# Moving a norm gain from the own inputs into the streamed weights, loading every input cast, and starting seven tiles together in PSUM

## The chip, the cores and the metric

One Trainium2 chip; the program runs on all 8 cores, four on each of two dies. Time is device time of the slowest core, in microseconds (us). Engines are named as in the profile: PE (TensorE; PEld its weight loads), DVE (VectorE), ACT (ScalarE), POOL (GpSimd), SP (SyncE, which only issues DMA here).

In a *slow* run one die has a visibly lower granted clock and the time is longer: in the first comparison, for one, die 1 at 0.887 to 0.896 and die 0 at 0.985 to 0.987, against all cores at 0.985 to 0.988.

## The reference, cut to what matters

```python
xn   = rmsnorm(x, g_in)                          # (x / rms(x)) * g_in
proj = einsum('bsd,de->bse', xn, w_in)           # 4096 -> 11840 columns
gB, gC, h, z_conv, c_q, c_kv, k_rope, z_attn = split(proj)
# gated short convolution from gB, gC, h, z_conv; latent attention from c_q, c_kv, k_rope, z_attn
out  = rmsnorm(x + concat(y_conv, y_attn) @ w_out, g_final)
```

Batch 2, sequence 4096, width 4096, fp32 in and out. Each core owns 1024 frames of one batch element. It needs `c_kv` and `k_rope` (512+64 columns, weights `WC`) for all 4096 frames of its batch element, as keys: 32 *tiles* of 128 frames, of which 8 are its *own*. All the other columns of `proj` it needs for its own frames alone: 88 *streamed weight tiles* of 4096x128. The row scale 1/rms(x) is applied after the matmuls. The gain `g_in` runs along the contracted dimension, so it can be multiplied into either x or the weights.

## The kernel before: the parts that matter

The kernel lists its instructions for each engine in program order, and in the traces each engine takes its own list in that order: in the changed kernel, on core 2, DVE stood 5.3 us for a table, up to 122.1 us, while an addition behind it in its list, whose input ACT had written by 110.5 us, started at 122.9 us. A helper derives the waits from what is read and written. One of its rules: an engine that reads a PSUM bank also waits for earlier reads of that bank by other engines.

```python
for k in rc:                                   # cells read; PSUM cells are whole banks
    ...
    if k[0] == "ps":
        for e2, r in c.r.items():              # other engines that have read this bank
            if e2 != eng:
                need(r)
```

First stage: every tile gives latent and rope columns and its sum of squares. `WC` is key weight times `g_in`. Other tiles (`a != 0`) are cast to bf16 by the DMA itself (`load("pool", ...)`). Own tiles come as fp32 through three small stages, because they are needed twice: cast, for the keys, and multiplied by `g_in`, as `XG`, for the streamed weights.

```python
def prep(T, c):                                # quarter c of tile T
    a, m = TILES[T]
    xt = xb[T % 4][:, 8 * c:8 * c + 8, :]
    src = xt
    if a == 0:                                 # own tile
        s = xst[nst[0] % 3]                    # three fp32 stages
        load("sp", s, x_tile[T, quarter c])
        tt(XG[own columns], s, g_in, ALU.mult) # DVE
        src = s
        act(xt, src, AF.Copy)                  # ACT: fp32 -> bf16
    act(q, src, AF.Square)                     # ACT
    tt(q[:, 0:512], q[:, 0:512], q[:, 512:1024], ALU.add)     # DVE: sums of squares,
    tt(o[:, :], q[:, 0:256], q[:, 256:512], ALU.add)          # reduced further by PE

def pe_main(T, kc):
    A, B = banks_of(T)                         # a pair of PSUM banks
    mm(psum[:, A, 0:256], x_, WC[:, kc, 0:256], kc == 0, kc == 31)
    mm(psum[:, B, 0:320], x_, WC[:, kc, 256:576], kc == 0, kc == 31)
```

Four other tiles run together while `WC` arrives. Then own and other tiles alternate (eight pairs), and other tiles close the stage. `post(T)` normalizes, `pe_trans(T)` transposes into the key buffers.

Second stage: streamed weights, cast on load into three buffers.

```python
def wload(i):
    for c in range(2):
        load("pool", WS[i % 3][half c], w_in_d[i, half c])
# 64 tiles of the convolution group, then 8 of c_q, then 16 of z_attn; the c_q part:
for m in range(8):
    for hf in range(2):
        for kc in range(32):
            mm(o, w[:, kc, :], XG[:, kc, c0:c0 + 512], kc == 0, kc == 31)
            if kc == 15 and pend:
                pend.pop(0)()                  # PE: ones x squares of the previous half
        ts(CQG[...], o, g_q, ALU.mult)         # DVE reads the bank
        act(s2, o, AF.Square)                  # ACT reads the same bank, after DVE
        pend.append(lambda: mm(bank(6 + hf), ones16, s2, ...))
    wload(64 + m + 3)
```

Attention and the output projection follow. The change doesn't touch them.

The softmax here doesn't subtract the row's maximum and nothing guards it: scores larger than these inputs give would overflow.

Of the kernel before, what the change touches and what calls it, by code (L numbers as in the profile page):

```python
# [15 lines left out]
D = 4096  # L16
# [68 lines left out]
class Prog:  # L85
# [15 lines left out]
    def add(self, eng, fn, reads=(), writes=(), dma=False):  # L101
# [23 lines left out]
        for k in wc:  # L125
            c = self.cells.get(k)
            if c is None:
                c = self.cells[k] = Cell()
            w = c.w
            if w is not None and (dma or w.dma_sem is not None or w.eng != eng or eng != "pe"):  # L130
                need(w)
            for e2, r in c.r.items():
                if dma or e2 != eng or eng == "pool":
                    need(r)
            for r in c.dr:
                need(r)
# [109 lines left out]
KB = 1024  # L246
# [15 lines left out]
def tile_order():  # L262

    own = [(0, t) for t in range(8)]
    oth = [(a, m) for a in (1, 2, 3) for m in range(8)]
    seq = oth[:4]
    rest = oth[4:]
    for t in range(8):
        seq += [own[t], rest[t]]
    return seq + rest[8:]  # L270
# [5 lines left out]
def build_program():  # L276
# [7 lines left out]
    x_tile = din("x_tile", [32, 128, 4096])  # L284
# [21 lines left out]
    with stack:  # L306
# [62 lines left out]
        def small(name, shape, dt=F32):  # L369
# [12 lines left out]
        stat = [small("stat%d" % i, [8]) for i in range(4)]  # L382
        fst = [small("fst%d" % i, [12]) for i in range(8)]
# [16 lines left out]
              enumerate((Z_R + 8 * KB, Z_R + 16 * KB, Z_Q + 36 * KB, Z_RB + 4352))]  # L400
        xst = [sb("xst%d" % i, o, [8, 128], F32) for i, o in enumerate((Z_R, Z_R + 4 * KB, Z_G + 28 * KB))]
        wst = [sb("wst%d" % i, Z_C + i * 4608, [2, 576], F32, Z_K2) for i in range(7)]
        sq = [sb("sq%d" % i, Z_T + i * 2 * KB, [1024], BF16) for i in range(2)]
        sa2 = [sb("sa2_%d" % i, Z_T + 4 * KB + i * 512, [256], BF16, Z_CONST) for i in range(6)]
        zc = [Z_RB + 4352 + 8 * KB]

        def ptmp(name, shape, dt=F32):
            n = int(np.prod(shape)) * (2 if dt == BF16 else 4)
            t = sb(name, zc[0], shape, dt, Z_T)
            zc[0] = (zc[0] + n + 63) // 64 * 64  # L410
            return t

        ckn = [ptmp("ckn%d" % i, [512], BF16) for i in range(2)]
        junk = ptmp("junk", [512], BF16)
        kr = [ptmp("kr%d" % i, [2, 64], BF16) for i in range(2)]
        ckn += [sb("ckn%d" % (2 + i), Z_K2 + 5 * KB + i * KB, [512], BF16) for i in range(2)]
        kr += [sb("kr%d" % (2 + i), Z_K2 + 7 * KB + i * 256, [2, 64], BF16) for i in range(2)]
        t1 = ptmp("t1", [64])
        t2 = ptmp("t2", [64])
        cst = [ptmp("cst%d" % i, [128]) for i in range(3)]  # L420
        gkv = ptmp("gkv", [512])

        def load_other(T, parts=2):
            n = 32 // parts
            for c in range(parts):
                load("pool", xb[T % 4][:, c * n:(c + 1) * n, :],
                     x_tile[T, :, c * n * 128:(c + 1) * n * 128].rearrange("p (k t) -> p k t", k=n))

        def load_cs(T):
            load("sp", cst[T % 3][:, :], cs_key[T])  # L430

        nsa = [0]
        nst = [0]
        saof = {}

        def prep(T, c):

            a, m = TILES[T]
            xt = xb[T % 4][:, 8 * c:8 * c + 8, :]
            src = xt  # L440
            if a == 0:
                s = xst[nst[0] % 3]
                nst[0] += 1
                load("sp", s[:, :, :], x_tile[T, :, c * 1024:(c + 1) * 1024].rearrange("p (k t) -> p k t", k=8))
                tt(XG[:, 8 * c:8 * c + 8, m * 128:(m + 1) * 128], s[:, :, :],
                   g_in[:, 8 * c:8 * c + 8].unsqueeze(2).to_broadcast([128, 8, 128]), ALU.mult)
                src = s[:, :, :]
                act(xt, src, AF.Copy)  # L448
            q = sq[nsa[0] % 2]
            o = sa2[nsa[0] % 6]  # L450
            saof[(T, c)] = o
            nsa[0] += 1
            act(q[:, :].rearrange("p (k t) -> p k t", k=8), src, AF.Square)
            tt(q[:, 0:512], q[:, 0:512], q[:, 512:1024], ALU.add)
            tt(o[:, :], q[:, 0:256], q[:, 256:512], ALU.add)

        def banks_of(T):
            return (2 * T, 2 * T + 1) if T < 4 else (2 * ((T - 4) % 3), 2 * ((T - 4) % 3) + 1)

        def pe_main(T, kc):  # L460
            A, B = banks_of(T)
            x_ = xb[T % 4][:, kc, :]
            mm(psum[:, A, 0:256], x_, WC[:, kc, 0:256], kc == 0, kc == 31)  # L463
            mm(psum[:, B, 0:320], x_, WC[:, kc, 256:576], kc == 0, kc == 31)  # L464

        def pe_ssq(T, c):
            B = banks_of(T)[1]
            s = saof[(T, c)]
            for j in range(2):
                mm(psum[:, B, 320:321], s[:, j * 128:(j + 1) * 128], ones16[:, 0:1], False, True)  # L470
            if TILES[T][0] == 0:
                for j in range(2):
                    mm(psum[:, B, 384:512], ones16[:, :], s[:, j * 128:(j + 1) * 128], False, True)

        def post(T):
            a, m = TILES[T]
            A, B = banks_of(T)
            st = stat[T % 4]
            cs = cst[T % 3]
            sx = psum[:, B, 320:321]  # L480
            lat = psum[:, A:A + 2, 0:256]
            act(junk[:, :].rearrange("p (b c) -> p b c", b=2), lat, AF.Square, accum=st[:, 0:1])
            act(st[:, 2:3], sx, AF.Sqrt, scale=1.0 / D, bias=EPSA)
            if a == 0:
                act(RB[:, m * 128:(m + 1) * 128], psum[:, B, 384:512], AF.Sqrt, scale=1.0 / D, bias=EPSA)
            ts(st[:, 1:2], sx, EPS / D, ALU.mult, EPS * EPS, ALU.add)
            recip(st[:, 4:5], st[:, 2:3])
            act(st[:, 3:4], st[:, 0:1], AF.Sqrt, scale=1.0 / 512, bias=st[:, 1:2])
            stt(t1[:, :], psum[:, B, 256:320], st[:, 4:5], cs[:, 0:64], ALU.mult, ALU.mult)
            stt(t2[:, :], psum[:, B, 256:320], st[:, 4:5], cs[:, 64:128], ALU.mult, ALU.mult)  # L490
            recip(st[:, 5:6], st[:, 3:4])
            stt(ckn[T if T < 4 else T % 2][:, :].rearrange("p (b c) -> p b c", b=2), lat, st[:, 5:6],  # L492
                gkv[:, :].rearrange("p (b c) -> p b c", b=2), ALU.mult, ALU.mult)
            k_ = kr[T if T < 4 else T % 2]
# [4 lines left out]
            if a == 0:  # L499
                recip(RB[:, m * 128:(m + 1) * 128], RB[:, m * 128:(m + 1) * 128])  # L500
            if T + 3 < 32:
                load_cs(T + 3)

        def pe_trans(T):
            a, m = TILES[T]
            b_ = 6 + T % 2
            pt = psum[:, b_, :].bitcast(BF16)
            for j in range(4):
                tr(pt[:, j * 128:(j + 1) * 128], ckn[T if T < 4 else T % 2][:, j * 128:(j + 1) * 128], id16[:, :])
            tr(pt[:, 512:640], kr[T if T < 4 else T % 2][:, :, :].rearrange("p a b -> p (a b)"), id16[:, :])  # L510
# [8 lines left out]
        for c in range(8):  # L519
            for T in range(4):  # L520
                load("pool", xb[T][:, 4 * c:4 * c + 4, :],
                     x_tile[T, :, c * 512:(c + 1) * 512].rearrange("p (k t) -> p k t", k=4))
        for i in range(16):
            w = wst[i % 7]
            load("sp", w[:, :, :], w_ckv_d[i].rearrange("p (k c) -> p k c", k=2))
            for j in range(2):
                ts(WC[:, 2 * i + j, :], w[:, j, :], g_in[:, 2 * i + j:2 * i + j + 1], ALU.mult)
            if i == 1:
                idst = sb("idst", Z_K2, [128])
                gmst = sb("gmst", Z_K2 + 512, [2, 64])  # L530
                load("sp", idst[:, :], ident_d)
                load("sp", gmst[:, :, :], gmask_d.rearrange("p (a b) -> p a b", a=2))
                load("sp", g_q[:, :], g_q_d)
                load("sp", convw[:, :], convw_d)
                load("sp", gkv[:, :], g_kv_d)
                ms(ones16[:, :], 1.0)
                ms(eps_t[:, :], EPS)
        cp(id16[:, :], idst[:, :])
        cp(gmask[:, :, :], gmst[:, :, :])
        for T in range(3):  # L540
            load_cs(T)


        for c in range(4):
            for kc in range(8 * c, 8 * c + 3):
                for T in range(4):
                    pe_main(T, kc)
            if c:
                for T in range(4):
                    pe_ssq(T, c - 1)  # L550
            for T in range(4):
                prep(T, c)
            for kc in range(8 * c + 3, 8 * c + 8):
                for T in range(4):
                    pe_main(T, kc)
        for T in range(4):
            pe_ssq(T, 3)

        def maybe_load(T):
            if T < 32 and TILES[T][0] != 0:  # L560
                load_other(T)

        for T in range(4, 8):
            maybe_load(T)
        for c in range(4):
            prep(4, c)
        for T in range(3):
            post(T)
        for T in range(4, 32):
            post(T - 1)  # L570
# [519 lines left out]
```

## Time and profile before

| | |
|---|---|
| time | 2930.11 us, median of 3 (2928.58 to 2936.37) |
| profiled run | 2937.51 us, fast; cores 2913.7 to 2936.0 us |
| first streamed-weight matmul | 436 to 455 us after the core's start, by core |
| from there to the end | 2475 to 2483 us on the four cores looked at |

The last two rows split the run at the start of the first matmul on a streamed weight tile, called *the handover* below. In the profile, a line with a source number (L644 here) gives the first and last start of its instructions.

The first view is windows of the slowest core (core 2): from:to, length, then for each engine busy us (instructions), then granted PE clock, DMA busy share and GB/s.

```profile
core 2: us, PE busy (x) PEld busy (x) DVE busy (x) ACT busy (x) POOL busy (x), PEclk, DMA share, GB/s
0.00:62.00 62.00, 19.46 (x88) 10.86 (x88) 14.82 (x33) 3.28 (x3) 17.46 (x36) 0.75 1.00 221
114.00:340.00 226.00, 143.59 (x1115) 107.84 (x1114) 110.58 (x296) 99.61 (x142) 8.98 (x17) 0.82 0.45 109
344.00:440.00 96.00, 94.29 (x877) 76.19 (x875) 60.94 (x221) 59.01 (x92) 12.69 (x24) 1.00 0.86 146
460.00:1712.00 1252.00, 1252.00 (x6772) 662.25 (x6771) 230.50 (x324) 77.88 (x108) 92.48 (x175) 1.00 0.47 78
```

The streamed weights (460 to 1712) are TensorE-bound: 1252 of 1252 us. In the pairs (114 to 340) TensorE is busy 64% of the time, and no engine nor the DMA is full. In the tail of other tiles (344 to 440) the same matmuls run at 94 of 96 us. So the pairs wait for something in series. The chain of waits of core 2 names it (start, length, engine or DMA, what):

```profile
114.37 6.95 DMA xst_75<-x_tile
121.40 1.06 ACT xb_72 L448
122.46 0.95 ACT sq_84 L453
123.48 8.56 DMA xst_75<-x_tile
...
148.66 6.96 DMA xst_76<-x_tile
```

A quarter of an own tile is loaded (7 us), cast and squared by ScalarE (2 x 1 us). Only then is its stage free for the next load (8.6 us), and so on. The same pattern recurs 34 us later: that is the period of a pair, against 8.2 us for one tile in the tail.

### The profile page before, as it was taken

What the parts mean: (1) busy time and instruction counts of PE and PEld (TensorE: products, weight loads), DVE (VectorE), ACT (ScalarE), POOL (GpSimd) and SP (SyncE); (2) the same over time, 40 slices, a digit from 0 to 9 for tenths busy, and PEclk for the clock granted to TensorE, in tenths of its full rate; (3) what the DMA queues carried; (4) which work ended last, traced back from release to release, by engine and by line L of the source; (5) the groups of instructions that cost most, each with busy time, mean ns of one, the idle gap of its engine ahead of it and who ended that gap; (6) DMA issues with size and microseconds to landing.
All of it is one profiled execution on the core that took longest, in us unless ns stands there. A gap on an engine that the chain in (4) does not pass through costs nothing.

```text
span 2936.0 us, 40663 instructions; the slowest of 8 cores (2913.7 to 2936.0 us)
## 1 busy us (share of the span) xinstructions
PE 2706.9 (92%) x15672; PEld 1494.5 (51%) x15672; DVE 1129.3 (38%) x2105; ACT 719.2 (24%) x1113; POOL 183.8 (6%) x348
## 2 busy tenths in 40 slices
PE   3766799999999999999999999999999989999993
PEld 2544575555555555554444455555555544444441
DVE  3544562221112112211121157878778782100134
ACT  1534560000000000000010045554545551100110
POOL 2000010000000000000000000000000000000100
PEclk7888899999999999999999999999999999999996
DMA  9444583444445444444445410010100056766658
GB/s 215 86 99 125 114 149 48 82 83 79 79 76 86 83 76 76 83 84 86 72 75 82 74 22 16 16 22 16 22 16 15 8 134 154 174 151 135 154 123 268
DMA packets 87757, 261.02 MB, mean 89 GB/s; under 512 B 10000, under 2 KB 18448, under 8 KB 86416
## 3 DMA queue, kind: packets, MB, share of 16 engines
q0 software_dynamic: 50560, 174.09, 35.2%
q1 hardware_dynamic: 37008, 84.34, 9.1%
q8 instruction: 127, 2.08, 0.3%
q14 instruction: 62, 0.51, 0.1%
HBM read 390.51 MB, written 31.46 MB: 144 GB/s over the span
## 4 chain that ended last, share of the span: by engine, by line
PE 76%; DVE 8%; DMA 8%; issue 4%; ACT 3%; DVEq 0%; SPq 0%; ACTq 0%; POOLq 0%
PE ps L644 31%; PE ps L934 13%; PE ps L710 8%; PE ps L694 4%; PE ps L769 3%; PE ps L760 3%; PE ps L464 3%; PE ps L898 3%; PE ps L825 3%; PE ps L824 3%; DVE ACC_148 L895 3%; PE ps L463 2%; DMA wst_78<-w_ckv 2%; DMA xst_75<-x_tile 1%; DMA xst_76<-x_tile 1%
## 5 line engine op out<-in xcount | busy, mean ns | idle before, releaser
L644 PE MATMUL ps<-XG,ws_110 128*128 128x384 bf16 (+2 forms) x1760 | 316.0, 341 | 3.9 <-DVE ckn_93 L492 3.9
L644 PE MATMUL ps<-XG,ws_111 128*128 128x384 bf16 (+2 forms) x1696 | 299.1, 338 | 0.0
L644 PE MATMUL ps<-XG,ws_112 128*128 128x512 bf16 (+2 forms) x1664 | 298.6, 341 | 0.0
L644 PEld LDWEIGHTS ps<-XG,ws_110 128*128 128x128 bf16 x1760 | 173.0, 98 | 143.2 <-issue 7.1
L644 PEld LDWEIGHTS ps<-XG,ws_111 128*128 128x128 bf16 x1696 | 165.8, 98 | 129.5
L644 PEld LDWEIGHTS ps<-XG,ws_112 128*128 128x128 bf16 x1664 | 162.8, 98 | 132.1
L824 PE MATMUL ps<-QN_136,KH_132 128*128 128x512 bf16 (+7 forms) x384 | 115.8, 318 | 0.0
L825 PE MATMUL ps<-TQ_138,K_64 128*128 128x512 bf16 (+7 forms) x384 | 115.8, 318 | 0.0
L825 PE MATMUL ps<-TQ_137,K_64 128*128 128x512 bf16 (+7 forms) x384 | 115.2, 317 | 0.0
L824 PE MATMUL ps<-QN_135,KH_131 128*128 128x512 bf16 (+7 forms) x384 | 115.2, 317 | 0.0
L883 ACT ACTIVATE PT_139<-ps 128x1024 bf16<-128x1024 f32 x96 | 84.6, 881 | 99.1 <-PE ps L825 99.1
L463 PE MATMUL ps<-WC,xb_70 128*128 128x256 bf16 x256 | 75.1, 309 | 30.3 <-DMA xb_70<-x_tile 11.4
L938 DVE TENSOR_TENSOR XR_165<-ps,XR_165 128x512 f32<-128x512 f32 x6 | 4.1, 691 | 248.1 <-PE ps L934 248.1
L883 ACT ACTIVATE PT_141<-ps 128x768 bf16<-128x768 f32 (+1 forms) x96 | 70.9, 739 | 107.9 <-PE ps L825 107.7
L883 ACT ACTIVATE PT_140<-ps 128x896 bf16<-128x896 f32 (+1 forms) x96 | 77.8, 810 | 72.6 <-PE ps L825 72.2
L463 PE MATMUL ps<-WC,xb_72 128*128 128x256 bf16 x256 | 73.6, 304 | 17.3 <-ACT xb_72 L448 11.4
L710 PE MATMUL ps<-XG,ws_110 128*128 128x512 bf16 x384 | 84.0, 379 | 0.0
L464 PE MATMUL ps<-WC,xb_70 128*128 128x320 bf16 x256 | 79.4, 342 | 0.0
L464 PE MATMUL ps<-WC,xb_72 128*128 128x320 bf16 x256 | 77.5, 336 | 0.0
L895 DVE TENSOR_TENSOR ACC_148<-ACC_148,PT_140 128x1024 f32<-128x1024 f32 (+1 forms) x64 | 65.6, 1025 | 18.8 <-ACT PT_140 L883 12.5
L883 ACT ACTIVATE PT_142<-ps 128x640 bf16<-128x640 f32 (+1 forms) x96 | 63.5, 661 | 33.4 <-PE ps L825 33.4
L710 PE MATMUL ps<-XG,ws_112 128*128 128x512 bf16 x320 | 69.9, 379 | 0.0
(470 smaller groups left out, 4348.3 us busy)
## 6 DMA issues: line engine op xcount, KB each, us to landing
ws_110<-w_in_t POOLq DMA_DIRECT2D x60, 512.0 KB, 5.8
ws_111<-w_in_t POOLq DMA_DIRECT2D x58, 512.0 KB, 5.8
ws_112<-w_in_t POOLq DMA_DIRECT2D x58, 512.0 KB, 5.7
xb_71<-x_tile POOLq DMA_DIRECT2D x14, 512.0 KB, 9.5
xb_73<-x_tile POOLq DMA_DIRECT2D x14, 512.0 KB, 8.7
xst_74<-x_tile SPq DMA_DIRECT2D x11, 512.0 KB, 7.7
xst_75<-x_tile SPq DMA_DIRECT2D x11, 512.0 KB, 7.8
xst_76<-x_tile SPq DMA_DIRECT2D x10, 512.0 KB, 7.8
```

Source lines behind the costliest of these rows:

```text
L463: mm(psum[:, A, 0:256], x_, WC[:, kc, 0:256], kc == 0, kc == 31)
L464: mm(psum[:, B, 0:320], x_, WC[:, kc, 256:576], kc == 0, kc == 31)
L644: mm(o, w[:, kc, :], XG[:, kc, c0:c1], kc == 0, kc == 31)
L694: mm(o, w[:, kc, :], XG[:, kc, c0:c0 + 512], kc == 0, kc == 31)
L710: mm(o, w[:, kc, :], XG[:, kc, c0:c0 + 512], kc == 0, kc == 31)
L760: mm(o, WQ[h % 2][:, kc, part * 128:(part + 1) * 128], CQG[:, kc, bi * 512:(bi + 1) * 512], kc == 0, kc == 7)
L769: mm(o, w[:, kc, (h % 2) * 128:(h % 2) * 128 + 128], CKVN[:, kc, s_ * 512:(s_ + 1) * 512], kc == 0, kc == 3)
L824: mm(o, KH[h % 2][:, k0:k0 + 128], QN[h % 2][:, c0:c0 + w], True, False)
L825: mm(o, K2[:, k0:k0 + 128], TQ[h % 2][:, c0:c0 + w], False, True)
L883: act(pt[:, :, 0:w], psum[:, 2 * (n % 2):2 * (n % 2) + 2, 0:w], AF.Exp, scale=ATTN_SCALE)
L895: tt(A, A, pt[:, :, 0:w], ALU.add)
L934: mm(bank(t_), src[:, kc % 16, t_ * 128:(t_ + 1) * 128], WO[slot][:, kcc, :], kc == 0, kc == 31)
```

## The change

Its intent: own tiles are loaded already cast, straight into `XG`, without a stage. This requires that `XG` no longer carry `g_in`, so the gain moves into the streamed weights. They then can't be cast by the DMA (one rounding is wanted, of weight times gain), so they arrive as fp32 quarters in three stages and DVE multiplies them. The first seven own tiles accumulate together in all eight PSUM banks while `WC` arrives, with their rope columns sharing one bank. A dependency rule also becomes stricter: ACT and DVE now wait for their own earlier reads before they overwrite. Cut to its core:

```diff
-            for e2, r in c.r.items():
-                if dma or e2 != eng or eng == "pool":
+                if dma or e2 != eng or eng != "pe":
                     need(r)
 def tile_order():
-    (4 other tiles, then 8 pairs of an own and another tile, then other tiles)
+    return [(0, t) for t in range(8)] + [(a, m) for a in (1, 2, 3) for m in range(8)]
 def prep(T, c):
-            if a == 0:  (stage load, XG multiply, cast)
-            act(q, src, AF.Square)
+            act(q, xtile(T)[quarter c], AF.Square)     # xtile: XG for own tiles, xb for others
 def banks_of(T):
-            return (2 * T, 2 * T + 1) if T < 4 else (2 * ((T - 4) % 3), 2 * ((T - 4) % 3) + 1)
+            return (T - 7) % 4, 7 - (T - 7) % 2
 def pe_main(T, kc):
-            mm(psum[:, A, 0:256], x_, WC[:, kc, 0:256], ...); mm(psum[:, B, 0:320], x_, WC[:, kc, 256:576], ...)
+            mm(psum[:, A, :], x_, WC[:, kc, 0:512], ...);     mm(psum[:, B, 0:64], x_, WC[:, kc, 512:576], ...)
 def pe_trans(T):                                       # four transposes of ckn and one of kr, then
+            if a == 0:                                 # row scale of own frames, broadcast by a matmul
+                ts(diag, id32, rown[:, T:T + 1], ALU.mult)            # DVE
+                mm(psum[:, b_, 384:512], ones32, diag, True, True)    # PE, fp32
+                cp(RB[own columns], psum[:, b_, 384:512])             # DVE
             (copies of the transposes to CKVN and K2: DVE)
+def wload(q):                                          # quarter of a streamed weight tile, fp32
+                load("sp", stg[q % 3], w_in_d[i, quarter c])
+def wmul(i):
+                for c in range(4):
+                    q = 4 * i + c
+                    tt(WS[i % 2][quarter c], stg[q % 3], g_in, ALU.mult)     # DVE
+                    wload(q + 3)
+        for c in range(8):                             # shared start of seven own tiles
+            (WC[...] = wst * g_in; next loads)
+            for kc in range(4 * c, 4 * c + 4):
+                for T in range(7):
+                    mm(psum[:, T, :], x_, WC[:, kc, 0:512], ...)
+                    mm(psum[:, 7, 64 * T:64 * T + 64], x_, WC[:, kc, 512:576], ...)
+            (squares of four kc of all seven tiles)
+        post_group((0, 1))                             # normalizes shared tiles 0 and 1: frees their banks
         for T in range(7, 32):
             (half of tile T's matmuls)
+            if T == 7: post_group((6, 2, 3, 4, 5))
             (prep of T+1; transposes: postponed ones of tiles 0..6 up to four a tile at T = 9..11; the other half; post(T))
```

## The prediction

> **What bounds the kernel now.** TensorE, except in the first stage (projection of all 32 key tiles to 576 latent and rope columns). In the windows view (core 2, slowest) TensorE is busy 100% from 460 to 1712 us (88 streamed weight tiles), 95% in the attention, 90% in the output projection, at a granted clock of 0.95-1.00. The first stage takes 454.8 us (first streamed-weight matmul in the timeline) at a clock of 0.5-0.9. The cores' spread (2914-2936 us) is already there when they leave it (436-455 us). Its parts:
> - 0-62 us: DMA share 1.0; 9.4 MB of key weights and 8.4 MB of x are read, about 290 GB/s.
> - 110-340 us: eight pairs of an own and another tile, about 33 us a pair. The chain of waits runs through the own tiles' fp32 stages: load 7-8 us, two ScalarE passes of 1.05 us, again a load; TensorE half idle.
> - 344-440 us: only other tiles, cast on load: TensorE full, 8.2 us a tile, DMA share 0.86.
>
> **What the change does.** Seven own tiles go straight into the bf16 tile, cast, and accumulate together in eight PSUM banks while weights arrive. Later tiles are cast and prefetched four deep, so the paired part should run like the third. Per tile TensorE does 512+64 columns instead of 256+320. In the timeline 512 columns take 216 ns start to start and 64 columns 30 ns (attention), together 0.246 us against 0.245: neutral. [...]
>
> Estimates from these durations:
> - Seven shared tiles: 14.7 MB x + 9.4 MB weights at 280-290 GB/s: ends about 88-90 us. TensorE's 55 us hide under it.
> - Tile 7 lands in 256-byte rows, queued behind the last own rows: 10-17 us instead of 7. TensorE resumes at about 103 us.
> - 25 tiles x 8.35 us (32 x 0.246 plus squares and transposes) = 209 us, plus 5 us for bank releases and delayed transposes: end near 318 us.
> - The handover gap (about 8 us idle, then half clock) mostly goes.
>
> Gain: 455-318 = about 137 us, all on the critical path.
>
> Added: the streamed weights (88 x 2.1 MB) load as fp32 in quarters through three stages; VectorE multiplies them by g_in. The same operation on own x took 1.22 us, so 4.9 us a weight tile, 430 us in all, in a stretch where VectorE is busy 18%. A weight tile lasts 14 us on TensorE; the next is ready about 7-8 us after its buffer comes free (the fourth quarter loads after the first multiply), despite two buffers instead of three. Off the critical path; I allow 3 us. Attention and output projection stay; own-engine waits on overwrites cost nothing visible.
>
> **Predicted: 2796 us, 2772 to 2835 in 8 of 10.** Faster by over 2%: 0.95; within 2%: 0.04; slower by over 2%: 0.01.
>
> **What would show it.** First streamed-weight matmul at 305-330 us, cores within 10 us; DMA share near 1 to about 90 us, then one TensorE gap of 8-20 us ended by tile 7's load; then 8.3-8.6 us a tile; TensorE full during the streamed weights, VectorE there at 45-55%; weight multiplies of 1.2 us; attention and output projection within 3 us of now.
>
> **What would make it wrong.** Fp32 quarters landing later than about 8 us, so that TensorE waits for VectorE at each weight tile (1 us each costs 88 us). The own tiles' cast load slower than estimated, or x lagging behind 8.35 us a tile with eight cores reading. [...]

455 - 318 = 137 us gained, less 3 us for the fold, takes 2930 us to 2796 us. Its 290 GB/s count the fp32 bytes that are read (17.8 MB in 62 us); the profile's column has 221 for the same stretch.

## The result

The first comparison, four timed runs a kernel: after 2852.62 us median (2821.77 to 3088.48), before 2930.12 us. Of the changed kernel's four runs two were fast, 2821.77 and 2835.37 us. The ratio of the fast runs is 0.965 (95% interval 0.960 to 0.970). A ratio here is the mean time of one kernel's fast runs over that of the other's fast runs of the same rounds, so it is not quite the ratio of the medians quoted. A second job with the changed kernel gave five fast runs (2817 to 2837 us) and 0.966.

| | before | after |
|---|---|---|
| fast runs | 2929 to 2936 us | 2822 and 2835; later 2817 to 2837 us |
| handover, by core | 436 to 455 us | 339 to 343 us; two cores 359 us |
| rest of the run (four cores) | 2475 to 2483 us | 2470 to 2477 us |

So all but some 5 us of the gain lies before the handover. After it nothing of size happened, although DVE's busy time there grew by 400 us. The attention takes as long as it did: on core 2 the time from the first score matmul to the first output-projection matmul is 723.6 us in the kernel before and 723.3 us in the changed one. The output projection after it takes 487 to 493 us before and 483 to 488 us after, by core; what makes it shorter on most cores is not shown.

Windows of core 2, which ran at the undisturbed clock; same columns as above:

```profile
0.00:95.00 95.00, 65.27 (x498) 32.16 (x499) 28.42 (x53) 26.80 (x9) 13.03 (x22) 0.91 1.02 200
95.00:165.00 70.00, 44.39 (x351) 24.25 (x350) 38.48 (x147) 29.13 (x51) 2.65 (x5) 0.85 0.60 102
165.00:340.00 175.00, 175.00 (x1631) 95.17 (x1630) 111.19 (x398) 105.39 (x166) 19.11 (x36) 1.00 0.73 126
345.00:1597.00 1252.00, 1252.00 (x6784) 663.10 (x6783) 627.23 (x681) 77.87 (x108) 2.65 (x5) 1.00 0.53 152
```

The shared start is DMA-bound (share 1.02) and ends at 95 us, seven tiles done. The tail from 165 us is TensorE-bound without a gap. The streamed weights are still TensorE-bound, now beside 627 us of DVE instead of 230. But between 95 and 165 us TensorE stands for 26 of 70 us. What it waited for between 90 and 180 us (engine, line, whom for: us in total, times, longest):

```profile
PE ps L531 <- DVE diag L530: 10.4, 5, 2.7
PE ps L470 <- DVE sa_4_85 L455: 9.2, 1, 9.2
PE ps L463 <- DVE ckn_95 L508: 4.5, 1, 4.5
```

All three end with DVE. At the third, DVE was waiting in its turn: in the chain of waits ScalarE copies and squares the banks (L612, L499) from 95.4 to 97.7 us before DVE can go on. The chain of waits of the same core shows why the longest one is so long:

```profile
112.65 0.66 DVE ckn_100 L508
113.77 8.20 DMA cst_90<-cs_key
122.06 0.28 DVE t_0_113 L513
...
123.01 0.34 DVE sq_79 L454
124.18 0.30 DVE sa_5_86 L455
```

DVE works through the group of shared tiles. For tile 6 it needs a rope table (`cst`) whose buffer, one of a ring of four, was only just freed by tile 2. It waits 5.3 us for that DMA, which takes 8.2 us from issue to landing while x tiles fill the DMA engines (share 1.04 from 110 to 120 us). The sums of squares of tile 8 (`sq`, `sa`), which TensorE wants, stand behind it in DVE's list.

A second thing is seen on core 6, the slowest of the profiled run: the same work, at a granted clock of 0.81 for part of the stage. In its chain of waits the transposes (L321) of successive tiles mark the time that a tile takes:

```profile
192.50 0.35 PE ps L321 x5
202.48 0.35 PE ps L321 x5
...
305.16 0.30 PE ps L321 x5
313.48 0.30 PE ps L321 x5
```

A tile takes 9.98 us at clock 0.81 and 8.32 us at 1.00. The clock records of this run have 144 us at 0.8125 on cores 6 and 7, and none on the other six, cores 4 and 5 of the same die included. From 270 us on both have 1.00 again. That is why these two hand over at 359 us, not at 339 to 343.

### The profile page after: what moved, and what is told of

Read it like the earlier page. It is cut to its first block, busy times and chain, and to the rows that moved or that the text cites. A ratio compares the mean times of both kernels' runs of the same rounds, so it can differ in the third digit from the quotient of the medians.

```text
span 2833.8 us, 40912 instructions; the slowest of 8 cores (2810.1 to 2833.8 us)
## 1 busy us (share of the span) xinstructions
PE 2688.2 (95%) x15392; PEld 1417.0 (50%) x15624; DVE 1476.8 (52%) x2381; ACT 681.8 (24%) x1044; POOL 87.2 (3%) x159
## 4 chain that ended last, share of the span: by engine, by line
PE 81%; DVE 7%; DMA 5%; issue 4%; ACT 3%; DVEq 0%; ACTq 0%; POOL 0%; POOLq 0%; SPq 0%
PE ps L699 32%; PE ps L991 14%; PE ps L766 8%; PE ps L463 6%; PE ps L825 3%; PE ps L750 3%; PE ps L816 3%; PE ps L954 3%; PE ps L881 3%; PE ps L880 3%; DVE ACC_163 L951 2%; DMA XG<-x_own 2%; PE ps L834 1%; DMA RR_205<-hsp 1%; PE ps L464 1%
## 5 line engine op out<-in xcount | busy, mean ns | idle before, releaser
L699 PE MATMUL ps<-XG,ws_122 128*128 128x384 bf16 (+2 forms) x2544 | 454.5, 339 | 0.8
L699 PE MATMUL ps<-XG,ws_121 128*128 128x384 bf16 (+2 forms) x2528 | 451.2, 339 | 2.5 <-DVE ws_121 L555 0.8
L699 PEld LDWEIGHTS ps<-XG,ws_121 128*128 128x128 bf16 x2560 | 250.3, 98 | 200.4 <-issue 1.2
L699 PEld LDWEIGHTS ps<-XG,ws_122 128*128 128x128 bf16 x2560 | 250.4, 98 | 199.6
L881 PE MATMUL ps<-TQ_153,K_60 128*128 128x512 bf16 (+7 forms) x384 | 115.9, 319 | 0.9
L881 PE MATMUL ps<-TQ_152,K_60 128*128 128x512 bf16 (+7 forms) x384 | 115.2, 317 | 0.9
L766 PE MATMUL ps<-XG,ws_121 128*128 128x512 bf16 x502 | 111.4, 379 | 0.5
L766 PE MATMUL ps<-XG,ws_122 128*128 128x512 bf16 x502 | 111.3, 379 | 0.5
L880 PE MATMUL ps<-QN_151,KH_147 128*128 128x512 bf16 (+7 forms) x367 | 109.5, 316 | 0.0
L880 PE MATMUL ps<-QN_150,KH_146 128*128 128x512 bf16 (+7 forms) x367 | 108.7, 314 | 0.0
L555 DVE TENSOR_TENSOR ws_121<-stg_125,g_in 128x1024 bf16<-128x1024 f32 x59 | 72.0, 1220 | 57.8 <-DMA stg_125<-w_in_t 57.4
L555 DVE TENSOR_TENSOR ws_122<-stg_124,g_in 128x1024 bf16<-128x1024 f32 x59 | 72.0, 1221 | 56.3 <-DMA stg_124<-w_in_t 56.3
L555 DVE TENSOR_TENSOR ws_122<-stg_123,g_in 128x1024 bf16<-128x1024 f32 x59 | 72.0, 1221 | 55.9 <-DMA stg_123<-w_in_t 55.7
L555 DVE TENSOR_TENSOR ws_121<-stg_123,g_in 128x1024 bf16<-128x1024 f32 x59 | 72.0, 1220 | 55.5 <-DMA stg_123<-w_in_t 55.5
L555 DVE TENSOR_TENSOR ws_121<-stg_124,g_in 128x1024 bf16<-128x1024 f32 x58 | 70.8, 1220 | 52.9 <-DMA stg_124<-w_in_t 52.9
L555 DVE TENSOR_TENSOR ws_122<-stg_125,g_in 128x1024 bf16<-128x1024 f32 x58 | 70.8, 1221 | 52.7 <-DMA stg_125<-w_in_t 52.7
L593 PE MATMUL ps<-WC,XG 128*128 128x512 bf16 x215 | 63.6, 418 | 28.8 <-DMA XG<-x_own 25.3
L766 PEld LDWEIGHTS ps<-XG,ws_122 128*128 128x128 bf16 x512 | 50.2, 98 | 60.3
```

Source lines behind the costliest of these rows:

```text
L555: tt(WS[i % 2][:, 8 * c:8 * c + 8, :], stg[q % 3][:, :, :], g_in[:, 8 * c:8 * c + 8].unsqueeze(2).to_broadcast([128, 8, 128]), ALU.mult)
L699: mm(o, w[:, kc, :], XG[:, kc, c0:c1], kc == 0, kc == 31)
L880: mm(o, KH[h % 2][:, k0:k0 + 128], QN[h % 2][:, c0:c0 + w], True, False)
L881: mm(o, K2[:, k0:k0 + 128], TQ[h % 2][:, c0:c0 + w], False, True)
```

## The experiments

The theory after reading the two traces: (1) the gain is the fp32 stages of the own tiles going away; (2) the fold is free; (3) the shared start is worth little as it stands, because it piles DVE work up behind it. The main rival: the shared start is what gained. Twelve runs were made, eleven variants and the changed kernel once more, each beside runs of the kernel before. All twelve were reported correct within the tolerance of the comparison. That includes the variants that leave `g_in` out somewhere: `g_in` is 1 with a standard deviation of 2%, so this comparison can't see it.

### cast_only: one part alone, the cast

```diff
 # kernel before
             if a == 0:
-                (fp32 stage; XG multiply from it; ACT copy)
+                tt(XG[own columns], xt, g_in, ALU.mult)      # DVE, from the cast tile
 def maybe_load(T):
-            if T < 32 and TILES[T][0] != 0:
+            if T < 32:
```

> The kernel before with one part of the change alone: its eight own tiles are cast on load and prefetched four deep like the others, and the own input for the later projections is made by VectorE from the cast tile times g_in. No fold into the weights, no shared PSUM, old tile order. Theory (the fp32 stages of the own tiles were most of the loss): a pair takes 16.7 us instead of 33, the first streamed-weight matmul comes at 350-362 us instead of 455 on the slowest core, and the time is 2825-2850 us. Rival (the shared PSUM start is what gained): a pair still takes over 25 us and the time stays above 2880 us.

Measured: fast runs 2855 to 2860 us, ratio 0.975 (0.973 to 0.978), handover at 371 to 378 us. That misses the theory's band by 5 to 10 us (the handover's by 9 us or more) and rules out the rival's (over 2880 us): the cast alone brings 75 of the 110 us or so. A pair now takes 20.1 us instead of 34. Why not 16.7? The chain of waits of core 2 in the pairs:

```profile
158.90 0.86 DVE RB L354
159.76 1.08 DVE XG L442
160.84 0.34 DVE sq L449
161.48 1.22 DVE XG L442
...
179.01 0.86 DVE RB L354
179.88 1.08 DVE XG L442
```

The multiply of own x by `g_in` is on the chain. It stands in DVE's list ahead of the sums of squares, 4 x 1.2 us a pair, with other DVE work around it.

### cast_direct: the cast without any multiply

```diff
 # kernel before
+        def xtile(T):                                   # own tiles are loaded straight into XG
+            return XG[:, :, m * 128:(m + 1) * 128] if a == 0 else xb[T % 4][:, :, :]
             if a == 0:
-                (everything)
```

No shared start, old order, `WC` as before, streamed weights as before: `g_in` is missing for own frames.

> The kernel before with the own tiles cast on load straight into the own input (rows of 256 bytes), with no multiply of own x at all and none of the streamed weights: everything of the change's first stage except the shared PSUM start and the new order. Its result lacks g_in in the streamed projections of own frames, on purpose. In the run with the cast alone a pair took 20.4 us and the streamed weights began at 371-375 us, with the multiply of own x in the chain of waits. Theory A (that multiply, on the same VectorE queue as the squares, is what the cast-only run still lacks; the shared PSUM gives little): a pair takes 17-18.5 us (256-byte rows cost 11.5 us of DMA a tile, so 18 us a pair is the DMA's floor), streamed weights at 340-357 us, time 2822-2840 us. Theory B (the shared PSUM start is worth the missing 30 us): a pair stays above 20 us, streamed weights at 365 us or later.

The 11.5 us are from the changed kernel's trace, core 2: the 4096 rows of 256 bytes of tile 7 took 45 ns each, 11.5 us of the 16 DMA engines together, and a tile in rows of 4096 bytes (409 ns each) 6.5 us. The 18 us a pair are the estimate, the sum of the two.

Measured: fast runs 2824 to 2831 us, ratio 0.965 (0.962 to 0.968), handover at 338 to 347 us. Theory A holds: this is the changed kernel's ratio (0.965) and nearly its handover (339 to 343 us), without a shared start. The pairs are full now:

```profile
114.00:330.00 216.00, 214.88 (x2010) 174.03 (x2008) 137.25 (x492) 131.11 (x209) 31.82 (x50) 1.00 0.94 137
```

The edit changes a second thing: own tiles no longer pass through the ring of four `xb` buffers. The waits of TensorE on core 2 up to 350 us tell the two apart. First cast_only, then cast_direct:

```profile
PE ps L458 <- DMA xb<-x_tile: 20.2, 6, 11.6
PE ps L326 <- DVE ckn L487: 17.6, 7, 3.0
```

```profile
PE ps L458 <- DMA xb<-x_tile: 19.9, 6, 9.8
PE ps L326 <- DVE ckn L487: 0.8, 1, 0.8
```

The waits for loads stayed; the waits for DVE in the pairs went.

So nearly all of the gain needs neither the shared start nor the new order. In undisturbed runs (no core at a lowered clock) the changed kernel is a little faster still: 2817 to 2822 us against 2824 to 2831, in different jobs. In its other fast runs (2834 to 2837 us) it is slower.

### cast_pool: the multiply of own x moved to GpSimd

```diff
 # cast_only
-                tt(XG[own columns], xt, g_in, ALU.mult)
+                tt(XG[own columns], xt, g_in, ALU.mult, "pool")
```

> The cast-only run with the multiply of own x moved from VectorE to GpSimd; all else the same, result correct. Theory A (the multiply hurts because VectorE does it in order ahead of the sums of squares that TensorE waits for): a pair takes 16.7-18.5 us, streamed weights at 338-357 us, time 2820-2840 us. Theory B (a start worth 30 us is missing, whoever multiplies): streamed weights stay at 365-375 us. GpSimd at over 4 us a quarter would spoil the test: then a pair takes over 17 us on GpSimd itself.

Measured: two fast runs at 2886 us, handover at 399 to 406 us: slower than cast_only by 30 us. Neither theory expected that, so the run doesn't decide between them. It shows something else. In the order of time on core 2:

```profile
141.16 7.46 POOL L442 TENSOR_TENSOR XG<-xb,g_in 128x1024 bf16<-128x1024 bf16 x4
143.31 0.75 DVE L487 SCALAR_TENSOR_TENSOR ckn<-ps,stat,gkv 128x512 bf16<-128x512 f32 x1
143.97 4.86 DVE L491 TENSOR_TENSOR kr<-t,t 128x64 bf16<-128x64 f32 x2
...
148.99 0.27 PE L326 MATMUL ps<-id,kr 128*128 128x128 bf16 x1 [4.40 <-DVE kr L491]
```

Four GpSimd multiplies of 1.9 us each run from 141.16 to 148.62 us. Two small DVE additions, which take 0.35 us together in cast_only, take 4.86 us here: they start inside that time, at 143.97 us, and end 0.2 us after it, at 148.83 us. TensorE waits 4.4 us for them. From 130 to 330 us such an addition takes 968 ns in the mean, against 217 ns in cast_only. Not every DVE instruction is held: the one just before (L487), which reads PSUM and starts at 143.31 us, takes its 0.75 us, as in cast_only; the two additions read SBUF alone. What holds them is not shown.

### no_fold: the changed kernel without the fold

```diff
 # changed kernel
 def wmul(i):
-                (four multiplies from fp32 stages)
+                for c in range(2):
+                    load("pool", WS[i % 2][half c], w_in_d[i, half c])
```

> The changed kernel without the fold: streamed weights are cast on load into the same two buffers, no fp32 stages, no multiply by g_in. Its result is wrong on purpose (g_in is missing in the streamed projections). Theory (the multiply is off the critical path): fast runs within 8 us of the changed kernel's 2822-2835 us, VectorE busy 430 us less. Rival (the multiply or the two buffers delay TensorE): 15 us or more faster.

Measured: two fast runs, 2818 and 2819 us, ratio 0.962 (0.959 to 0.965), handover at 337 to 343 us. The changed kernel's fast runs with no core at a lowered clock are 2817 to 2822 us. The theory holds: 430 us of DVE multiplies and the second buffer instead of a third cost nothing that can be seen.

How much room there is shows in the changed kernel, core 2, in the order of time:

```profile
905.88 1.22 DVE L555 TENSOR_TENSOR ws_122<-stg_125,g_in 128x1024 bf16<-128x1024 f32 x1
...
908.15 1.22 DVE L555 TENSOR_TENSOR ws_122<-stg_124,g_in 128x1024 bf16<-128x1024 f32 x1
911.40 1.23 DVE L555 TENSOR_TENSOR ws_122<-stg_125,g_in 128x1024 bf16<-128x1024 f32 x1 [2.03 <-DMA stg_125<-w_in_t]
```

Three quarters were ahead, the fourth landed 2 us later, and the tile was ready at 912.6 us. TensorE took it at 917.8 us: 5.2 us to spare.

### mul2 and mul3: how far the fold is from hurting

```diff
 # changed kernel, wmul
+                    for _ in range(2):                  # mul3: range(3)
                         tt(WS[i % 2][quarter c], stg[q % 3], g_in, ALU.mult)
```

> The changed kernel with each multiply of the streamed weights done twice (same result). VectorE then needs 9.8 us a weight tile instead of 4.9, of 14 us that TensorE takes. Theory (slack of some 6 us): still ready in time, fast runs within 8 us of 2822-2835 us, VectorE 430 us busier. Rival (the fold is already at its limit): over 40 us slower.

Measured: four fast runs, 2839 to 2842 us, ratio 0.969: some 20 us slower than the changed kernel undisturbed. The expectation (within 8 us) failed, and the rival's (over 40 us) wasn't met either. On core 2 the first score matmul comes 1284 us after the handover, instead of 1264 us. TensorE's longest waits there:

```profile
PE ps L757 <- ACT sq L756: 14.8, 8, 3.3
...
PE ps L767 <- DVE ws L556: 1.7, 3, 0.6
```

It hardly waited for weights (`ws`, 1.7 us), so the slack for the weights themselves was there. It waited once in each of the eight `c_q` tiles for ACT's squares. The matmul of the squares of one half stands in the middle of the next half; ACT's square waits for DVE's read of the same bank; DVE's read stands behind the multiplies of the next weight tile. The expectation had counted only when a weight tile is ready, not what else is queued behind the multiplies.

> As the run before with each multiply done three times: 14.7 us of multiplies and 2 to 4 us of evictions a weight tile, over the 14 us of TensorE. Theory: VectorE becomes the limit of this stage, 150 to 400 us slower. If it is not slower, the model of VectorE as the next limit is wrong.

Measured: four fast runs, 3231 to 3248 us, about 410 us slower than the changed kernel, a little over the band. As expected, TensorE waits for the weights:

```profile
PE ps L700 <- DVE ws L556: 209.8, 127, 2.7
PE ps L757 <- ACT sq L756: 66.0, 8, 16.9
PE ps L767 <- DVE ws L556: 38.8, 27, 9.3
```

These are 315 us. Nearly all of the rest is slower matmuls: on core 2, from the handover to the first score matmul, all of TensorE's waits (320 us) taken off the 1676 us leave 1356 us here instead of 1264 us, with the same work. Over the whole run core 2's mean granted clock is 0.959, instead of 0.986 in the changed kernel.

### after_again, cst7, cst7_diag, spread: giving the shared start its worth

Four kernels on one chip, each adding to the one before.

```diff
 # cst7: changed kernel, seven rope tables instead of a ring of four for the shared tiles
+        cst_g = cst + [sb("cstg%d" % i, ...) for i in range(3)]
+            if c == 5:                                  # in the shared start, behind the last weights
+                for T in range(7): load_cs(T)
 # cst7_diag: and the diagonal one own tile ahead
-                ts(diag, id32, rown[:, T:T + 1], ALU.mult)
                 mm(psum[:, b_, 384:512], ones32, diag, True, True)
                 cp(RB[own columns], psum[:, b_, 384:512])
+                if T < 7: ts(diag, id32, rown[:, T + 1:T + 2], ALU.mult)
 # spread: and the postponed transposes at two a tile
-                if c == 0 and 8 < T < 12: trans(T, 1)
-                if 8 < T < 12 or T == 8 and c == 3: trans(T, 1)
+                if c == 3 and 8 <= T < 16: trans(T, 1)
```

> The changed kernel unchanged, as the yardstick on this chip for the three runs after it: fast runs 2815-2835 us, streamed weights at 338-343 us on undisturbed cores, ratio to before 0.962-0.966.

> The changed kernel with seven rope-table buffers for the seven shared tiles, all loaded before they are needed, instead of a ring of four. In the changed kernel's trace VectorE stood 5 us for the table of tile 6 (8 us from issue to landing) and TensorE 9 us for sums of squares queued behind it. Theory (that wait alone costs its length): streamed weights 6-9 us earlier, time 6-9 us less. Rival (the next thing in VectorE's queue takes its place): under 3 us.

> As cst7, and the diagonal matrix that carries an own tile's row scale is made one tile ahead, so that TensorE's fp32 matmul no longer waits for VectorE (10 us in five waits in the changed kernel). Theory: 6-10 us less than cst7, streamed weights at 322-328 us. Rival (VectorE's queue as a whole limits tiles 8 to 12, whose four postponed transposes each carry about 5 us of copies): under 3 us less than cst7.

> As cst7_diag, with the postponed transposes of the seven shared tiles spread at two a tile over tiles 9 to 15 instead of up to four a tile over 9 to 11. Theory (after the waits are gone, VectorE's queue is overfull in tiles 9 to 11): 4-10 us less than cst7_diag, streamed weights at 312-322 us, near the 318 us of the prediction. If it gains under 3 us, the rest of the loss is in the handover at 95-100 us and the throttled clock after it.

Measured. "Undisturbed" are the fast runs in which no core's mean clock is below 0.983; handovers are of cores whose clock is undisturbed.

| | fast runs | ratio (95%) | undisturbed runs | handover |
|---|---|---|---|---|
| after_again | 2817 to 2837, 5 of 6 | 0.966 (0.962 to 0.969) | 2817, 2817 | 336 to 341 |
| cst7 | 2812 to 2849, 6 of 7 | 0.965 (0.960 to 0.969) | 2812 to 2814 (three) | 334 to 339 |
| cst7_diag | 2811 to 2826, 5 of 5 | 0.963 (0.961 to 0.965) | 2811 | 330 to 333 |
| spread | 2803 to 2823, 6 of 6 | 0.962 (0.960 to 0.965) | 2803, 2804 | 321 to 327 |

The ratios' intervals overlap; the order is carried by the handovers, which are measured core by core. In the mean over these cores they move 2, then 5, then 8 us. The first step is not clear of the scatter between cores; after_again itself came within 2 us of its expectation.

- cst7: 2 us, the rival's figure, not the 6 to 9 us of the theory. The 9.2 us wait shrank to 3.8 us, but TensorE's waits for the diagonal grew from 10.4 to 12.1 us: the next thing in DVE's list took its place.
- cst7_diag: 5 us, between the two expectations (6 to 10, under 3). The waits for the diagonal fell from 12.1 to 6.3 us. They didn't go.
- spread: 8 us, as the theory said, though its band for the handover (312 to 322 us) is missed by up to 5 us. No wait for the diagonal is left.

The same stretch of core 2 in spread (it was 44.39 of 70 us in the changed kernel), and its two longest waits of PE from 90 to 180 us:

```profile
95.00:165.00 70.00, 60.48 (x506) 33.39 (x517) 48.56 (x187) 40.75 (x71) 5.31 (x10) 0.90 0.81 127
```

```profile
PE ps L464 <- DVE ckn L509: 4.5, 1, 4.5
PE ps L471 <- DVE sa L456: 4.5, 2, 4.0
```

So TensorE is busy 16 us more in this stretch, and the handover comes 15 us earlier. It was neither a single load nor a single wait, but the order in DVE's list. That the list was overfull, as the expectation says, is not shown: in the changed kernel DVE was busy only 38.5 of these 70 us. Between 90 and 180 us it stood 9.9 us itself for TensorE's fp32 matmuls (L531), and for ScalarE and the table besides. What TensorE wanted stood in order behind entries that were waiting. spread is correct, beats both kernels, and hands over near the 318 us of the prediction.

### spread_split and direct_512: what lowers the clock

Of the changed kernel's seven fast runs, four have two or four cores at a mean clock of 0.975 to 0.979 instead of 0.985 to 0.988, each 15 to 20 us longer, always in neighbouring pairs (0 and 1, 2 and 3, ...). cst7, cst7_diag and spread show it too; cast_only and cast_direct showed it in none of three fast runs each. Two kernels were to tell whether the shared start or the 512+64 columns bring it on.

```diff
 # spread_split: spread, with tiles 7 to 31 on 256+320 columns in three pairs of banks (and tile 6 normalized first)
-            mm(psum[:, A, :], x_, WC[:, kc, 0:512], ...);     mm(psum[:, B, 0:64], x_, WC[:, kc, 512:576], ...)
+            mm(psum[:, A, 0:256], x_, WC[:, kc, 0:256], ...); mm(psum[:, B, 0:320], x_, WC[:, kc, 256:576], ...)
 # direct_512: cast_direct, with the opposite edit
```

> The run with the spread transposes, with tiles 7 to 31 on 256+320 columns in three pairs of banks, as in the kernel before, instead of 512+64 (the seven shared tiles stay 512+64). Undisturbed time as in that run (2800-2810 us, streamed weights at 320-328 us). Question: about half of the fast runs of the kernels with the shared start have one or more pairs of cores at a granted clock of 0.81 for about 144 us of the first stage, 15-20 us longer, which no run of the kernel before has shown. Theory S (the shared start, dense from the beginning, brings it on): it appears here too, in 2 or more of the fast runs. Theory C (the 512+64 matmuls bring it on): it appears in none here.

> The run with own tiles cast straight into place (no shared start, old order), with 512+64 columns instead of 256+320. Undisturbed time as in that run (2820-2832 us, streamed weights at 336-345 us), since 512+64 takes TensorE 0.246 us against 0.245. Theory S (the shared start brings on the 0.81 stretch): no pair of cores shows it in fast runs here. Theory C (the 512+64 matmuls): pairs of cores at a mean clock about 0.01 lower and 15-20 us longer in 2 or more of the fast runs.

Measured: only two and three of six runs each were fast, spread_split at 2802 and 2803 us, direct_512 at 2821 to 2824 us. No core has the lower clock in these five. The expectation for theory C fits spread_split and that for theory S fits direct_512, so they contradict each other, and the counts are too small: the question stays open. Of the four slow runs of spread_split two have a pair of cores at 0.977 to 0.979 on the die that wasn't slow, and one of the three of direct_512 has such a pair at 0.975, more than 20 us longer than that die's other two cores. So a pair's clock was lower without a shared start too. And none of the six fast runs of no_fold and mul2, which have the shared start, shows it, though one slow run of no_fold does. These runs came from several chips; whether the chip matters was not tested. The premise was also too strong: one fast run of the kernel before in this job (2945 us) had die 0 at 0.960 instead of 0.971. What the two runs do show is that the column split doesn't matter: direct_512 is within the range of cast_direct or 3 us below it, and spread_split equals spread's undisturbed runs.

## Why the prediction was right or wrong

The predicted 2796 us (2772 to 2835) against fast runs of 2822 and 2835 us: the change is faster, by about 100 us instead of 134. The range holds the first and ends at the second (2835.37 us, 0.4 us outside); the median of all four, slow runs included, 2852.62 us, is outside it.

- **"The chain of waits runs through the own tiles' fp32 stages."** Right. cast_only takes away only that and gains 75 us; cast_direct shows nearly all the rest of the gain to be the multiply of own x on the same DVE list, about 30 us more.
- **"Per tile TensorE does 512+64 columns instead of 256+320 ... neutral."** Right: 8.32 us a tile measured against 8.35 predicted, and direct_512 equals cast_direct. In the trace of the kernel before, 64 columns take 30 ns from start to start and 512 take 216 ns.
- **"Seven shared tiles ... ends about 88-90 us."** 95 us, 5 to 7 us low.
- **"Tile 7 lands in 256-byte rows ... TensorE resumes at about 103 us", "one TensorE gap of 8-20 us ended by tile 7's load."** Wrong in mechanism. That load was issued at 80.5 us and landed 12.9 us later, before the shared start ended; its 256-byte rows took 11.5 us of the 16 DMA engines, against 6.5 us for a later tile in 4096-byte rows. The gap was 4.5 us and was ended by DVE's `ckn`, which frees the bank. TensorE resumed at 99.8 us; that this is near the predicted 103 us is luck.
- **"... plus 5 us for bank releases and delayed transposes."** This is the term that was mis-sized. On core 2 it is what is left of the 240.5 us from 99.8 us to the handover at 340.3 us when 25 x 8.32 us are taken off: 32 us instead of 5. TensorE stood for 21 of them (the 26 us between 95 and 165 us without the gap of 4.5 us). The other 11 us hold the postponed transposes and matmuls at a lowered clock (mean 0.85 from 95 to 165 us) and were not told apart. The handover came at 339 to 343 us, not 318. cst7, cst7_diag and spread take 15 us of it back by changing what stands in DVE's list there.
- **"The handover gap mostly goes."** Right: TensorE is busy 175 of 175 us up to 340 us, without a wait at the handover and at clock 1.00. In the kernel before, core 2's TensorE waits 3.9 us there (not about 8) and has a clock of 0.50 from 455 to 458 us.
- **"Off the critical path; I allow 3 us"** for the fold. Right: no_fold's two fast runs (2818 and 2819 us) lie within the undisturbed runs of the changed kernel (2817 to 2822 us). The tile is ready 9 us after its buffer is free, not 7-8 us, so there are 5 us of slack. mul2 shows that they don't hold for the `c_q` tiles, where other DVE work is behind the multiplies.
- **A lower granted clock.** Named as a risk, with a cause that is not shown. It came in four of seven fast runs of the changed kernel (two or four cores at 0.975 to 0.979 in the mean), at 15 to 20 us. What sets it off was not found.
- **"Cores within 10 us"** at the handover: 4 us on the six undisturbed cores, 20 us with the two at a lower clock.
- **"Own-engine waits on overwrites cost nothing visible."** Not tested alone. The attention, where the stricter rule applies as well, took the same time within 0.3 us on core 2. The output projection, also forecast within 3 us, is 8.5 us shorter there.

Where the gain came from, then: the own tiles' stages and their multiply left the first stage. The fold makes the second half of that possible, and pays with DVE time in a stage where DVE has room (busy 627 of 1252 us with it). The shared start finished seven tiles by 95 us, and the changed kernel gave nearly all of that back in the next 70 us. no_fold and cast_direct together suggest that the fold on top of cast_direct would be about as fast as the changed kernel; it was not run.

## What to carry to other kernels

An operation can be cheap in one stage and dear in another (the multiply by `g_in`: about 30 us on own x, nothing that can be seen on the streamed weights): ask whose list it stands in, and what waits behind it there. Where work is started in a group, its post-processing falls due in a group too; cost the engine that does it for the tiles right after the group, not as an average. When one wait is removed and the time moves by a small part of it, look at the engine's whole list before removing the next.
